# Scan layer: x and B of groups three to seven turned by VectorE blocks and DMAs through DRAM instead of by TensorE

## The chip, the cores and the metric

The kernel runs on one core of one Trainium2 chip. The metric is the device time of one execution in microseconds (us), taken as the median of several runs. TensorE (PE) multiplies matrices, VectorE (DVE) and ScalarE (ACT) do elementwise work, GpSimd (POOL) and SyncE (SP) issue DMAs here. Each engine works through its own instruction list in order; an instruction that waits for another engine or for a DMA holds up everything behind it on its engine.

## What is computed

Two residual layers and a final norm on a 512 x 1024 activation in f32. The first layer is a scan layer (SSD), the second an attention layer (MLA). The change touches the first one alone, cut here to what matters:

```python
proj = u @ in_w                                   # 1024 -> z (2048), x (2048), B (1024), C (1024), dt (32)
xbc  = silu(causal_depthwise_conv(proj[x, B, C]))
xdt  = x * dt                                     # heads of 64, 4 heads to a group, 8 groups, state 128
# in chunks of 128 positions, group by group:
cb     = C @ B^T                                  # per chunk
y_diag = (cb * decay) @ xdt
states = B^T @ (decay_to_end * xdt)               # one 128 x 64 state per head and chunk
y_off  = C @ (state entering the chunk) * exp(a_cum)
out    = gated_group_rms_norm(y_diag + y_off + d_skip * x, z) @ out_w
```

## The kernel before

**Layout.** Activations are kept turned: channels on the 128 partitions, the 512 positions along the free axis. Every product of the large projections is made in three passes (`whi*ah`, `whi*al`, `wlo*ah`) of 8 matmuls of 128x512, 24 matmuls for one 128-column slice of a weight. ACT casts a weight slice to its high part (`whi`, L272) and DVE subtracts to get the low part (`wlo`, L273). There are two `raw` buffers for loaded slices, three for `whi` and three for `wlo`; so the cast of a slice waits until the product two slices before the one now starting has ended, and it stands at the start of a product.

**Groups.** The scan runs over 8 groups, `g` = 0 to 7 (the first to the eighth). While the scan work of group g is done, TensorE's main feed is the projection of group g+1 (`ssm_in`): six products of 24 matmuls in the order B, C, x0, x1, z0, z1. When a product has ended, ACT reads its result (L608) and DVE adds three shifted multiples (the convolution, L610, three dependent steps).

**Order of the work.** TensorE's order is the order of the program. `sched` (L237) walks through the feed, counts 0.216 us for a matmul, and puts in the scan's pieces where the count passes the piece's number: `P1 = (1.0, 2.4, 3.8, 12.0, 18.2)` for `cb`, `x(0)`, `x(1)`, `states` and `y`; the group's norm (`gnorm`, the matmuls `pssq`) of the group before stands at 16.84. The count goes up in steps of 1.296 (six matmuls); 12.0 is passed after 60 matmuls. On the other engines, the DMA queues among them, a scheduler decides the order when the kernel is built.

**The scan's pieces for a group** (class `SSD`): `cb` (L64) turns three 128x128 blocks of B on TensorE (L71) into PSUM, ACT copies them out as `BT` (L73), then C·B (L77), the mask, and the product with the four decay tiles `L` (L81). `x(j)` (L83) turns four blocks of x on TensorE (L89); DVE multiplies by dt straight out of PSUM (`xdt`, L92) and by the decay to the end (`xw`, L94). `states` (L98) is three matmuls `aux<-xw,BT` (L105), followed by five short DVE operations for the running state `S` (L109 to L113). `y` (L116) is the products with `S` (L130) and with `xdt` (L138), and DVE's sums.

**DMAs.** SP issues all loads: weight slices (512 KB, L263), the broadcast rows `L<-ac_d` (L627) and `E<-ea_d` (L123, L124). In the second layer the program already turns a 512 x 1024 tensor in the way that the change uses: eight 128x512 operations that turn 32x32 blocks on DVE (L681), each followed by four DMAs of 64 KB that put the blocks in their places in DRAM (L684, pieces of 32 numbers, 128 bytes).

Of the kernel before, what the change touches and what calls it, by code (L numbers as in the profile page):

```python
# [10 lines left out]
F32 = mybir.dt.float32  # L11
# [4 lines left out]
P = 128  # L16
T = 512
D = 1024
KD = D // P
NCH = T // P  # L20
# [17 lines left out]
SU = (0.64, 1.42)  # L38
P0 = (6.0, 6.8, 11.91, 15.25, 17.25, 24.88, 34.5)
P1 = (1.0, 2.4, 3.8, 12.0, 18.2)  # L40
GN = 16.84
G7 = 33.0
SF = (0.02, 0.1, 2.1, 3.1)
# [11 lines left out]
class SSD:  # L55
# [8 lines left out]
    def cb(self):  # L64
        nc, net, wk, v = self.nc, self.net, self.wk, self.nc.vector
        B, C = self.st["B"], self.st["C"]
        ch = lambda ap: ap.rearrange("p (c s) -> p c s", c=NCH)
        pb = net.ssd_aux()
        for c in range(3):
            s = slice(c * P, (c + 1) * P)  # L70
            nc.tensor.transpose(pb[:, s], B[:, s], net.ident)  # L71
        self.BT = wk.tile([P, 3 * P], F32, tag="BT", name=net.nm("BT"), bufs=1)
        nc.scalar.copy(self.BT[:], pb[:, :3 * P])  # L73
        pc = net.ssd_aux()
        for c in range(NCH):
            s = slice(c * P, (c + 1) * P)
            nc.tensor.matmul(pc[:, s], B[:, s], C[:, s], start=True, stop=True)  # L77
        cb = wk.tile([P, T], F32, tag="cb", name=net.nm("cb"), bufs=2)
        v.tensor_tensor(ch(cb[:]), ch(pc[:]), net.triu[:, None, :].to_broadcast([P, NCH, P]), op=ALU.mult)
        for L in self.L:  # L80
            v.tensor_tensor(L[:], L[:], cb[:], op=ALU.mult)  # L81

    def x(self, j):  # L83
        nc, net, wk, v = self.nc, self.net, self.wk, self.nc.vector
        x = self.st[f"x{j}"]
        px = net.ssd_aux()
        for c in range(NCH):
            s = slice(c * P, (c + 1) * P)
            nc.tensor.transpose(px[:, s], x[:, s], net.ident)  # L89
        h0 = 4 * self.g + 2 * j  # L90
        xp = wk.tile([P, NCH, 2, 64], F32, tag="xdt", name=net.nm("xdt"), bufs=2)
        v.tensor_tensor(xp[:], px[:].rearrange("p (c h d) -> p c h d", c=NCH, h=2),  # L92
                        self.dt[:, :, h0:h0 + 2].unsqueeze(3).to_broadcast([P, NCH, 2, 64]), op=ALU.mult)
        v.tensor_tensor(self.xw[:, :, 2 * j:2 * j + 2, :], xp[:, :3],  # L94
                        self.dend[:, :3, h0:h0 + 2].unsqueeze(3).to_broadcast([P, 3, 2, 64]), op=ALU.mult)
        self.xdt.append(xp)
# [55 lines left out]
class Net:  # L152
# [8 lines left out]
    def build(self):  # L161
        tc, nc, ctx = self.tc, self.nc, self.ctx
        pool = lambda name, bufs, **k: ctx.enter_context(tc.tile_pool(name=name, bufs=bufs, **k))
        self.const = pool("const", 1)
        self.wraw = pool("wraw", 2)
        self.whi = pool("whi", 3)
        self.wlo = pool("wlo", 3)
        self.act = pool("act", 8)
        self.o16 = pool("o16", 16)
        self.nrm = pool("nrm", 1)  # L170
        self.res = pool("res", 8)
        self.dram = pool("dram", 1, space=bass.MemoryType.DRAM)

        const = self.const
        self.xs = []
        self.cols = const.tile([P, C_N], F32, name="cols")
        self.ident = const.tile([P, P], F32, name="ident")[:]
        self.rows = const.tile([P, 2 * NH], F32, name="rows")

        self.phase, self.group, self.before, self.head = "", [], [], None  # L180
        self.wq = []
        self.wpos = self.wload = 0
        self.wraws = []
        self.wready = {}
        for g in range(NG):
            for i in range(6):
                self.wq.append(("w", U_IN + 6 * g + i))
        for i in range(16):
            self.wq.append(("w", U_OUT0 + i))
        for i in range(6):  # L190
            self.wq.append(("w", U_M1 + i))
        self.wq += [("w", U_MZ + i) for i in range(3)] + [("ua", 0), ("w", U_MZ + 3), ("ub", 0), ("uc", 0), ("w", U_MZ + 4)]
        out = [("w", U_OUT1 + i) for i in range(16)]
# [12 lines left out]
        with tc.tile_pool(name="ps_m", bufs=1, space=bass.MemoryType.PSUM, reuse_waits="tile") as ps, \  # L206
                tc.tile_pool(name="mla", bufs=2, reuse_waits="tile") as wk:
            self.ps, self.wk = ps, wk
            self.mla()
# [50 lines left out]
    def load_weight(self, kind, idx):  # L260
        n = {"w": 1024, "ua": 1024, "ub": 640, "uc": 512}[kind]
        raw = self.wraw.tile([P, n], F32, tag="raw", name=self.nm("raw"))
        self.nc.sync.dma_start(raw[:], self.t[kind][idx])  # L263
        return raw

    def split_weight(self, raw, cuts=()):
# [70 lines left out]
    def sumsq(self, tiles, n, pstag, pool=None, tags=("r0", "rt", "rr"), after=None):  # L337
        nc = self.nc
        acc = None
        for x in tiles:  # L340
            sq = self.nrm.tile([P, T], F32, tag="sq", name=self.nm("sq"), bufs=SQ)
            i = nc.scalar.activation(sq[:], x, AF.Square)
            if after is not None:
                self.link(i, [after])
            if acc is None:
                acc = self.nrm.tile([P, T], F32, tag="sqa", name=self.nm("sqa"))
                nc.vector.tensor_scalar(acc[:], sq[:], self.eps_of(n), None, op0=ALU.add)
            else:
                nc.vector.tensor_tensor(acc[:], acc[:], sq[:], op=ALU.add)
        pool = pool or self.nrm  # L350
        hi = pool.tile([P, T], F32R, tag=tags[0], name=self.nm("sqh"))
        lo = pool.tile([P, T], F32R, tag=tags[1], name=self.nm("sql"))
        nc.scalar.copy(hi[:], acc[:])
        nc.vector.tensor_tensor(lo[:], acc[:], hi[:].bitcast(F32), op=ALU.subtract)
        ps = self.ps.tile([P, T], F32, tag=pstag, name=self.nm("pssq"), bufs=self.bufs[pstag])
        nc.tensor.matmul(ps[:], self.onesr[:], hi[:], start=True, stop=False)
        nc.tensor.matmul(ps[:], self.onesr[:], lo[:], start=False, stop=True)
        return ps[:]

    def ssm(self):  # L360
        tc, nc, t, wk = self.tc, self.nc, self.t, self.wk
# [33 lines left out]
        for k in range(KD):  # L395
            a = self.o16.tile([P, T], F32R, tag="o", name=self.nm("vh"))
# [32 lines left out]
            ul.append(b)  # L429

        gn = []
        self.silus(0)
        for g in range(NG):
            ys, q = [], []
            pieces = [] if g == 0 else [(GN, late)]
            if g == 0:
                begin = lambda: q.append(SSD(self, 0, self.lexp(0), ys))
                pieces += [(SU[0] + SU[1] * k, scaled) for k in range(KD)]
                pieces += [(P0[0], step), (P0[1], step), (P0[1] + 0.1, begin)]
                at = P0[2:]  # L440
            else:
                q.append(SSD(self, g, self.lexp(g), ys))
                at = P1
            pieces += [(at[0], lambda: q[0].cb()), (at[1], lambda: q[0].x(0)), (at[2], lambda: q[0].x(1)),
                       (at[3], lambda: q[0].states()), (at[4], lambda: q[0].y())]
            if g + 1 < NG:
                mid = (vh, vl, lambda: r, MID) if g == 0 else (uh, ul, None, 0)
                self.sched(self.ssm_in(g + 1, uh, ul, mid), pieces)
                self.silus(g + 1)
                late = functools.partial(lambda g, ys: gn.extend(self.gnorm(g, ys)), g, ys)  # L450
            else:
                self.part = []
                pieces.append((G7, lambda: gn.extend(self.gnorm(g, ys))))
                self.sched(self.out_half(gn, 0, U_OUT0, [t["x"][k] for k in range(KD)]), pieces)
# [616 lines left out]
```

## Time and profile before

| | |
|---|---|
| time, median of 3 runs | 836.59 us (835.94 to 836.82) |
| the profiled execution | 836.13 us; its span, first to last instruction, 834.0 us |
| busy: PE | 819.3 us, 98% of the span |
| busy: DVE | 644.9 us, 77% |
| busy: ACT | 450.4 us, 54% |
| busy: POOL | 0.2 us |
| granted TensorE clock, mean | 0.999 |

How to read the views in what follows. A row of the timeline has the start in us, the duration, the engine, the line of the kernel, the operation, output<-inputs, and `xN` where N equal operations follow each other (then the duration runs from the first start to the last end). What stands in brackets is the idle time of the engine before the row and what ended it. Durations overlap a little on DVE and ACT: a next operation that does not depend on the last starts about 0.08 us before its end. In the chain of waits a row has start, duration and work. Lines are those of the kernel before.

### The profile page before, as it was taken

To read this page: it belongs to the slowest core of one execution; us is meant where nothing else is said; L and a number is where in the kernel's file an instruction comes from. 1 tells how busy PE (TensorE), PEld (TensorE's weight loads), DVE (VectorE), ACT (ScalarE), POOL (GpSimd) and SP (SyncE) were. 2 spreads that over 40 slices of the span, in tenths; PEclk is the share of its full clock that TensorE was granted. 3 is DMA by queue.
4 is the path that set the end of the run, shared out by engine and by line. 5 is a ranking of instruction groups with operands and counts; after the bars stand their busy time and mean duration, and the time that the engine had idled before them with its cause. 6 is when DMAs were issued, how large, how long until landed. Compare 5 with 4: busy or idle time off the path is not lost.

```text
span 834.0 us, 11549 instructions
## 1 busy us (share of the span) xinstructions
PE 819.3 (98%) x4228; PEld 691.8 (83%) x4228; DVE 644.9 (77%) x1234; ACT 450.4 (54%) x794; POOL 0.2 (0%) x4
## 2 busy tenths in 40 slices
PE   7999999999999999999999999999999999999996
PEld 5887888888888888888888888888888888888885
DVE  7999898979787989778566787786767869675544
ACT  7567755545465657434353654556547557554233
POOL 0000000000000000000000000000000000000000
PEclk9999999999999999999999999999999999999999
DMA  6364543423242423333555142222222224331212
GB/s 227 103 191 141 155 147 106 152 99 129 101 139 90 152 76 127 115 121 94 130 130 132 54 130 64 79 72 76 63 64 58 90 78 152 101 97 56 86 66 101
DMA packets 50856, 90.55 MB, mean 109 GB/s; under 512 B 21552, under 2 KB 23088, under 8 KB 50800
## 3 DMA queue, kind: packets, MB, share of 16 engines
q1 hardware_dynamic: 50080, 88.77, 34.0%
q10 hardware_dynamic: 720, 1.05, 0.3%
q8 instruction: 33, 0.54, 0.3%
q14 instruction: 23, 0.19, 0.1%
HBM read 83.12 MB, written 4.33 MB: 105 GB/s over the span
## 4 chain that ended last, share of the span: by engine, by line
PE 92%; DVE 3%; DMA 2%; ACT 1%; SPq 1%; issue 0%; DVEq 0%; ACTq 0%
PE mm L291 55%; PE ot L941 11%; PE s L793 5%; PE mm L300 4%; PE po L835 4%; PE mm L773 3%; PE pt L817 2%; PE yd L138 2%; PE yd L291 1%; PE aux L130 1%; PE aux L105 1%; DMA x<-in_x_dram 1%; PE aux L77 1%; PE aux L89 1%; DMA L<-ac_d 1%; DVE wlo L273 1%
## 5 line engine op out<-in xcount | busy, mean ns | idle before, releaser
L272 ACT CAST whi<-raw 128x1024 fp32r<-128x1024 f32 (+3 forms) x132 | 127.0, 965 | 210.3 <-PE mm L291 172.8
L273 DVE TENSOR_TENSOR wlo<-raw,whi 128x1024 fp32r<-128x1024 f32 (+3 forms) x132 | 146.8, 1115 | 54.6 <-ACT whi L272 54.3
L291 PE MATMUL mm<-ah,whi 128*128 128x512 f32 x384 | 154.0, 401 | 0.0
L291 PE MATMUL mm<-ah,wlo 128*128 128x512 f32 x384 | 150.3, 391 | 0.4 <-DVE wlo L273 0.4
L291 PE MATMUL mm<-al,whi 128*128 128x512 f32 x384 | 149.9, 390 | 0.0
L291 PE MATMUL mm<-vh,whi 128*128 128x512 f32 x224 | 89.4, 399 | 0.8 <-ACT whi L272 0.8
L291 PE MATMUL mm<-vh,wlo 128*128 128x512 f32 x224 | 87.9, 392 | 0.7 <-DVE wlo L273 0.7
L291 PE MATMUL mm<-vl,whi 128*128 128x512 f32 x224 | 87.6, 391 | 0.0
L291 PEld LDWEIGHTS mm<-ah,wlo 128*128 128x128 f32 x384 | 72.1, 188 | 16.1 <-DVE wlo L273 0.8
L291 PEld LDWEIGHTS mm<-ah,whi 128*128 128x128 f32 x384 | 72.2, 188 | 15.3 <-issue 1.4
L291 PEld LDWEIGHTS mm<-al,whi 128*128 128x128 f32 x384 | 72.2, 188 | 14.4 <-DVE al L312 0.3
L941 PE MATMUL ot<-whi,ah 128*128 128x512 f32 (+1 forms) x136 | 52.4, 385 | 0.0
L941 PE MATMUL ot<-whi,al 128*128 128x512 f32 (+1 forms) x136 | 51.5, 379 | 0.0
L941 PE MATMUL ot<-wlo,ah 128*128 128x512 f32 (+1 forms) x136 | 51.4, 378 | 0.0
L291 PEld LDWEIGHTS mm<-vh,wlo 128*128 128x128 f32 x224 | 42.1, 188 | 10.7 <-DVE wlo L273 1.5
L291 PEld LDWEIGHTS mm<-vh,whi 128*128 128x128 f32 x224 | 42.2, 188 | 9.4 <-ACT whi L272 1.1
L223 ACT ACTIVATE p<-p,st 128x128 f32<-128x128 f32 (+1 forms) x64 | 36.1, 564 | 25.3 <-DVE st L805 25.2
L291 PEld LDWEIGHTS mm<-vl,whi 128*128 128x128 f32 x224 | 42.2, 188 | 7.3
L821 ACT CAST ph<-pt 128x512 fp32r<-128x512 f32 (+1 forms) x64 | 26.4, 421 | 33.3 <-PE pt L817 32.8
L291 PE MATMUL mm<-ch,whi 128*128 128x512 f32 x104 | 42.6, 410 | 0.0
L291 PE MATMUL mm<-ch,wlo 128*128 128x512 f32 x104 | 40.9, 393 | 0.0
L291 PE MATMUL mm<-cl,whi 128*128 128x512 f32 x104 | 40.8, 392 | 0.0
(223 smaller groups left out, 1637.7 us busy)
## 6 DMA issues: line engine op xcount, KB each, us to landing
raw<-in_w_dram SPq DMA_DIRECT2D x100, 512.0 KB, 3.3
L<-ac_d SPq DMA_DIRECT2D x32, 256.0 KB, 3.9
E<-ea_d SPq DMA_DIRECT2D x32, 128.0 KB, 3.5
raw<-in_ua_dram SPq DMA_DIRECT2D x8, 512.0 KB, 3.3
raw<-in_ub_dram SPq DMA_DIRECT2D x8, 320.0 KB, 2.8
x<-in_x_dram SPq DMA_DIRECT2D x8, 256.0 KB, 4.4
res<-in_x_dram SPq DMA_DIRECT2D x8, 256.0 KB, 3.1
hd<-ht SPq DMA_DIRECT2D x32, 64.0 KB, 3.5
```

The lines of the kernel that those rows point to most:

```text
L138: nc.tensor.matmul(yd[64 * h:64 * h + 64, s], self.xdt[j][:, c, h, :], self.L[2 * j + h][:, s], start=True, stop=True)
L223: i = self.nc.scalar.activation(out, in_, func, **k)
L272: nc.scalar.copy(hi[:, a:b], raw[:, a:b])
L273: nc.vector.tensor_tensor(lo[:, a:b], raw[:, a:b], hi[:, a:b].bitcast(F32), op=ALU.subtract)
L291: self.nc.tensor.matmul(ps, a, b, start=i == 0, stop=i == len(seq) - 1)
L300: self.nc.tensor.matmul(p, seq[i][0], seq[i][1], start=i == 0, stop=i == 3 * ks - 1)
L773: nc.tensor.matmul(ps[:, c2 * 256:(c2 + 1) * 256], a, b, start=i == 0, stop=i == 5)
L793: nc.tensor.matmul(ps[:, :n], x[:, s], y[:, :n], start=k == 0, stop=k == 4)
L817: nc.tensor.transpose(pt[:, (b - kb) * P:(b - kb + 1) * P], probs[h][b][:, kb * P:(kb + 1) * P], self.ident)
L821: nc.scalar.copy(ph[:, :n], pt[:, :n])
L835: nc.tensor.matmul(po[:, kb * P:], x, y, start=kb == 0 and k == 0, stop=kb == NCH - 1 and k == 2)
L941: nc.tensor.matmul(ps[:, a:b], x, y, start=start and i == 0, stop=stop and i == 5)
```

## The change

In groups g = 2 to 6 (the third to the seventh) TensorE no longer turns B and x. Instead:

- `flip` turns 32x32 blocks of x0, x1 and B on DVE (three operations of 128x512) and sends each with four DMAs of SP to a scratch tensor in DRAM, so that the blocks land in turned order: 12 DMAs, in pieces of 128 bytes;
- `back` reads the scratch with three DMAs of SP into `xdt` (two) and `BT`; ACT's copy of `BT` goes;
- `x(j)` multiplies `xdt` in place, from SBUF and not from PSUM;
- the pieces have other numbers: `P2` for groups four to seven, `P3` for the third, in which `states` is put at 15.5 and 19.0 (12.0 before), `y` at 21.0 and 25.0 (18.2 before). 15.5 is passed after 72 matmuls, which is the end of the product x0; 19.0 after 90;
- from the feed of group 1 on, all weight slices to the end of the program are issued by GpSimd (`wqueue`) and not by SP.

```diff
+P2 = (0.2, 1.0, 8.0, 11.5, 11.6, 15.5, 21.0)
+P3 = (0.2, 1.0, 8.0, 13.0, 13.1, 19.0, 25.0)
+FLIP = range(2, 7)
...
     def cb(self):
...
+        if self.g not in FLIP:
...
+    def flip(self):
+        nc, net, wk = self.nc, self.net, self.wk
+        d = net.flip_d[self.g % 2]
+        turned = d[:].rearrange("(j a) n -> a j n", a=32)
+        for m, name in enumerate(("x0", "x1", "B")):
+            t = wk.tile([P, T], F32, tag="u", name=net.nm("tp"), bufs=3)
+            nc.vector.transpose(t[:], self.st[name][:])
+            for i in range(4):
+                n = m * P + 32 * i
+                nc.sync.dma_start(turned[:, :, n:n + 32], t[32 * i:32 * i + 32, :].rearrange("a (j n) -> a j n", n=32))
+
+    def back(self):
+        nc, net, wk = self.nc, self.net, self.wk
+        rows = net.flip_d[self.g % 2][:].rearrange("(c p) n -> p c n", p=P)
+        self.px = []
+        for j in range(2):
+            xp = wk.tile([P, NCH, 2, 64], F32, tag="xdt", name=net.nm("xdt"), bufs=2)
+            nc.sync.dma_start(xp[:].rearrange("p c h d -> p c (h d)"), rows[:, :, j * P:(j + 1) * P])
+            self.px.append(xp)
+        self.BT = wk.tile([P, 3 * P], F32, tag="BT", name=net.nm("BT"), bufs=1)
+        nc.sync.dma_start(self.BT[:].rearrange("p (c n) -> p c n", c=3), rows[:, :3, 2 * P:])
...
     def x(self, j):
...
+        else:
+            xp = self.px[j]
+            px = xp[:]
+        v.tensor_tensor(xp[:], px,
...
-        self.nc.sync.dma_start(raw[:], self.t[kind][idx])
+        self.wqueue.dma_start(raw[:], self.t[kind][idx])
...
+        self.flip_d = [self.dram.tile([T, 3 * P], F32, name=f"flip{i}") for i in range(2)]
...
+                if g in FLIP:
+                    turn, cb, back, *rest = P3 if g == FLIP[0] else P2
+                    at = (cb, *rest)
+                    pieces += [(turn, lambda: q[0].flip()), (back, lambda: q[0].back())]
...
+            if g >= FLIP[0] - 1:
+                self.wqueue = nc.gpsimd
```

The order of the built programs at three places follows. A row has the line, the operation, output<-inputs with buffer numbers, and the shape. Lines are those of the program that the row is from: in the changed kernel `xdt` is L123, `xw` L125, `states` L136, the convolution L649, `wlo` L305, `pssq` L388 and the first step of the norm after it L354.

**TensorE, fifth group, around `states`.** Before: the product x0 of the next group is `mm_2136`, and the states stand within it, after 12 of its 24 matmuls.

```order
L291 MATMUL mm_2136<-al_563,whi_2096 128x512
L291 MATMUL mm_2136<-ah_562,wlo_2097 128x512
L105 MATMUL aux_2149<-xw_2024,BT_2042 128x256 x2
L105 MATMUL aux_2150<-xw_2024,BT_2042 128x256
L291 MATMUL mm_2136<-ah_595,whi_2096 128x512
```

Now: the product x0 is `mm_2152`, the product x1 `mm_2205`.

```order
L323 MATMUL mm_2152<-al_695,whi_2106 128x512
L323 MATMUL mm_2152<-ah_694,wlo_2107 128x512
L136 MATMUL aux_2186<-xw_2038,BT_2133 128x256 x2
L136 MATMUL aux_2187<-xw_2038,BT_2133 128x256
L323 MATMUL mm_2205<-ah_521,whi_2148 128x512
```

The states moved from the middle of the product x0 to the point between x0's last matmul and x1's first.

**VectorE, fifth group, around `xdt` and `xw`.** Before: the decay tiles, the four operations, then the low part of a weight and the convolution of the product B.

```order
L81 TENSOR_TENSOR L_2017<-L_2017,cb_2049 128x512
L92 TENSOR_TENSOR xdt_2066<-aux_2061,dt 128x512
L92 TENSOR_TENSOR xdt_2080<-aux_2075,dt 128x512
L94 TENSOR_TENSOR xw_2024<-xdt_2066,dec 128x3x128
L94 TENSOR_TENSOR xw_2024<-xdt_2080,dec 128x3x128
L273 TENSOR_TENSOR wlo_2133<-raw_2094,whi_2132 128x1024
L610 SCALAR_TENSOR_TENSOR B_2089<-mm_2031,cols,B_2089 128x511
```

Now: `whi_2261` is the cast that waits for the end of the product x0, and `x_389` is what the convolution makes of that product.

```order
L649 SCALAR_TENSOR_TENSOR C_2141<-mm_2110,cols,C_2141 128x509
L305 TENSOR_TENSOR wlo_2262<-raw_2199,whi_2261 128x1024
L649 SCALAR_TENSOR_TENSOR x_389_2181<-mm_2152,cols,x_389_2181 128x511
L649 SCALAR_TENSOR_TENSOR x_389_2181<-mm_2152,cols,x_389_2181 128x510
L123 TENSOR_TENSOR xdt_2129<-xdt_2129,dt 128x512
L649 SCALAR_TENSOR_TENSOR x_389_2181<-mm_2152,cols,x_389_2181 128x509
L125 TENSOR_TENSOR xw_2038<-xdt_2129,dec 128x3x128
L123 TENSOR_TENSOR xdt_2131<-xdt_2131,dt 128x512
L125 TENSOR_TENSOR xw_2038<-xdt_2131,dec 128x3x128
L140 COPY S_2191<-aux_2186 128x256
```

The four operations moved from ahead of the convolution of B to behind the low part and two steps of the convolution that belong to the end of the product x0.

**VectorE, third group, the same four operations.** Before they stand as in the fifth group.

```order
L92 TENSOR_TENSOR xdt_1350<-aux_1345,dt 128x512
L92 TENSOR_TENSOR xdt_1364<-aux_1359,dt 128x512
L94 TENSOR_TENSOR xw_1308<-xdt_1350,dec 128x3x128
L94 TENSOR_TENSOR xw_1308<-xdt_1364,dec 128x3x128
L273 TENSOR_TENSOR wlo_1417<-raw_1378,whi_1416 128x1024
```

Now: `x_259` comes from the product x0 of the next group; `rt_1486` waits for the norm's matmuls `pssq`, which TensorE has after the first six matmuls of the product x1, and for two operations of ACT on them.

```order
L305 TENSOR_TENSOR wlo_1534<-raw_1458,whi_1533 128x1024
L649 SCALAR_TENSOR_TENSOR x_259_1453<-mm_1424,cols,x_259_1453 128x511
L649 SCALAR_TENSOR_TENSOR x_259_1453<-mm_1424,cols,x_259_1453 128x510
L354 SCALAR_TENSOR_TENSOR rt_1486<-pssq_1482,r_270_1485 128x512
L123 TENSOR_TENSOR xdt_1401<-xdt_1401,dt 128x512
L123 TENSOR_TENSOR xdt_1403<-xdt_1403,dt 128x512
L125 TENSOR_TENSOR xw_1310<-xdt_1401,dec 128x3x128
L125 TENSOR_TENSOR xw_1310<-xdt_1403,dec 128x3x128
```

They moved behind the first step of the norm. In the fourth group all four stand between the third step of C's convolution and the `wlo` that waits for the end of x0; in the sixth and seventh the `xdt` and `xw` of x0 stand early, about the `L` products, and only those of x1 stand at C's convolution: on either side of its third step (sixth), or right behind it (seventh). The states of these three groups stand on TensorE as in the fifth, those of the third group after 18 matmuls of the product x1.

More of the change, by code (lines that the diff above doesn't have):

```diff
@@ L67, in cb @@
         ch = lambda ap: ap.rearrange("p (c s) -> p c s", c=NCH)
[L68 to L73, printed above, removed]
+        if self.g not in FLIP:
+            pb = net.ssd_aux()
+            for c in range(3):
+                s = slice(c * P, (c + 1) * P)
+                nc.tensor.transpose(pb[:, s], B[:, s], net.ident)
+            self.BT = wk.tile([P, 3 * P], F32, tag="BT", name=net.nm("BT"), bufs=1)
+            nc.scalar.copy(self.BT[:], pb[:, :3 * P])
         pc = net.ssd_aux()
@@ L81, in cb @@
             v.tensor_tensor(L[:], L[:], cb[:], op=ALU.mult)
+    def flip(self):
[16 more added lines that the diff above has]
+            self.px.append(xp)
+        self.BT = wk.tile([P, 3 * P], F32, tag="BT", name=net.nm("BT"), bufs=1)
+        nc.sync.dma_start(self.BT[:].rearrange("p (c n) -> p c n", c=3), rows[:, :3, 2 * P:])
     def x(self, j):
@@ L85, in x @@
         x = self.st[f"x{j}"]
[L86 to L89, printed above, removed]
         h0 = 4 * self.g + 2 * j
-        xp = wk.tile([P, NCH, 2, 64], F32, tag="xdt", name=net.nm("xdt"), bufs=2)
-        v.tensor_tensor(xp[:], px[:].rearrange("p (c h d) -> p c h d", c=NCH, h=2),
+        if self.g not in FLIP:
+            px = net.ssd_aux()
+            for c in range(NCH):
+                s = slice(c * P, (c + 1) * P)
+                nc.tensor.transpose(px[:, s], x[:, s], net.ident)
+            px = px[:].rearrange("p (c h d) -> p c h d", c=NCH, h=2)
+            xp = wk.tile([P, NCH, 2, 64], F32, tag="xdt", name=net.nm("xdt"), bufs=2)
+        else:
+            xp = self.px[j]
+            px = xp[:]
+        v.tensor_tensor(xp[:], px,
                         self.dt[:, :, h0:h0 + 2].unsqueeze(3).to_broadcast([P, NCH, 2, 64]), op=ALU.mult)
@@ L180, in build @@
         self.phase, self.group, self.before, self.head = "", [], [], None
+        self.wqueue = nc.sync
         self.wq = []
```

## Prediction

> **What bounds the kernel now.** I read first the page's span, busy times and chain, then who made TensorE (PE) wait, then the chain of waits through the fifth group.
>
> ```profile
> span 834.0 us, 11549 instructions
> PE 819.3 (98%) x4228; PEld 691.8 (83%) x4228; DVE 644.9 (77%) x1234; ACT 450.4 (54%) x794; POOL 0.2 (0%) x4
> ```
>
> ```profile
> PE mm L300 <- ACT whi L272: 4.8, 1, 4.8
> ...
> PE aux L105 <- DVE xw L94: 0.6, 1, 0.6
> ```
>
> TensorE is busy for 98% of the span, and the largest wait is the start-up (4.8 us, once). The states (L105) waited for DVE's `xw` once, for 0.6 us. So TensorE's list of work is the time, and two things count: matmul time taken off it is won in full, and a wait put into it is paid in full. The chain through the fifth group, start and duration:
>
> ```profile
> 211.38 0.33 PE aux L71 x3
> ...
> 214.00 0.43 PE aux L89 x4
> ...
> 215.82 0.44 PE aux L89 x4
> ...
> 225.82 1.30 PE aux L105 x6
> 227.12 4.10 PE mm L291 x18
> 231.22 0.23 PE pssq L356
> 231.45 0.23 PE pssq L357
> ...
> 251.50 0.33 PE aux L71 x3
> ```
>
> The turning of B (L71) and of x0 and x1 (L89) lies on the chain. One 128x512 matmul takes 4.10/18 = 0.228 us, a product of 24 takes 5.47. A group lasts 251.50 - 211.38 = 40.1 us; the turning of B stands six matmuls behind its start, which is 210.0. DVE's side of the same group is read from the timeline, ACT's casts beside it:
>
> ```profile
> 216.79 1.28 DVE L92 TENSOR_TENSOR xdt<-aux,dt 128x512 f32<-128x512 f32 x2
> 217.99 1.02 DVE L94 TENSOR_TENSOR xw<-xdt,dec 128x384 f32<-128x384 f32 x2
> ...
> 220.06 2.31 DVE L610 SCALAR_TENSOR_TENSOR B<-mm,cols,B 128x511 f32<-128x511 f32 x3
> 223.99 1.23 DVE L273 TENSOR_TENSOR wlo<-raw,whi 128x1024 fp32r<-128x1024 f32 x1 [1.62 <-ACT whi L272]
> 225.13 1.53 DVE L610 SCALAR_TENSOR_TENSOR C<-mm,cols,C 128x511 f32<-128x511 f32 x2
> 226.72 0.42 DVE L109 COPY S<-aux 128x256 f32<-128x256 f32 x1
> ...
> 230.75 1.23 DVE L273 TENSOR_TENSOR wlo<-raw,whi 128x1024 fp32r<-128x1024 f32 x1 [1.16 <-ACT whi L272]
> 231.89 1.53 DVE L610 SCALAR_TENSOR_TENSOR x<-mm,cols,x 128x511 f32<-128x511 f32 x2
> 233.34 0.68 DVE L322 SCALAR_TENSOR_TENSOR rt<-pssq,r 128x512 f32<-128x512 f32 x1
> 233.93 0.74 DVE L610 SCALAR_TENSOR_TENSOR x<-mm,cols,x 128x509 f32<-128x509 f32 x1
> 234.59 0.68 DVE L323 TENSOR_TENSOR rt<-rt,r 128x512 f32<-128x512 f32 x1
> ```
>
> ```profile
> 222.90 1.05 ACT L272 CAST whi<-raw 128x1024 fp32r<-128x1024 f32 x1 [3.71 <-PE mm L291]
> ...
> 229.66 1.05 ACT L272 CAST whi<-raw 128x1024 fp32r<-128x1024 f32 x1 [5.03 <-PE mm L291]
> ```
>
> The reader is to see three things. `xw` was ready at 219.0, about 7 us ahead of the states. A `wlo` is not free to run early: DVE stood idle for 1.62 and 1.16 us ahead of two of them, since the cast waits for the end of a product (222.90 is the end of C, 229.66 the end of x0). And the copy L109 sits between the second and third step of C's convolution, which is its place in the built program's list too: DVE keeps its list, whatever is ready behind.
>
> **What is removed.** Per group 0.33 + 0.43 + 0.44 = 1.20 us of TensorE, in five groups 6.0 us. ACT's copy of `BT` is off the chain and is worth nothing.
>
> **What is added on DVE and the queues.** The second layer has both new operations:
>
> ```profile
> L681 DVE STREAM_TRANSPOSE ht<-res x8: 699/711/712, 388.2 to 431.6; 128x512 f32<-128x512 f32 x8
> ```
>
> ```profile
> L684 SPq DMA_DIRECT2D hd<-ht x32: 341/487/856, 389.0 to 448.9; - x32
> ...
> DMA to landing us min/median/max: 2.3/3.5/3.7
> ```
>
> ```profile
> 213.00:253.00 40.00, 40.00 (x216) 33.58 (x215) 34.04 (x61) 22.20 (x35) 0.00 (x0) 1.00 0.35 119
> ```
>
> ```profile
> L<-ac_d SPq DMA_DIRECT2D x32, 256.0 KB, 3.9
> ```
>
> Three turns of 0.71 us are 2.1 us a group on a DVE that is busy for 34.04 of 40.00 us: there is room. A round trip is 3 x 0.71 on DVE, 12 issues of 0.49 = 5.9 us on SP, 3.5 to land, and 3.9 for the read (256 KB, as `L`): 15.4 us one after the other, and it starts about at the group's start (the operands are ready by then; in the fifth group the turns stand on DVE ahead of `cb`). The first `xdt` is read on DVE 16.2 us after the group's start at the earliest (C's end 222.90 - 210.0, less the 1.2 removed, and 4.46, below), and `BT`, the last to land, is needed later still; the issues also overlap the turns and each other's landing. I take 0, with a cover of a few us. Queued behind it on SP are only `L` and `E`, which need the group before to have finished, and weight slices no longer stand there. The multiplication by dt from SBUF instead of PSUM I take at the same 0.68 us.
>
> **What is added on TensorE: waits for `xw`.** The states need all of `xw`. I follow DVE's new list with the rows above.
>
> *Fifth group.* The states stand right behind the product x0, and DVE has the `wlo` of x0's end and two convolution steps of x0 ahead of `xdt`. From that end (229.66 in the rows): `wlo` starts at +1.09; the convolution at +2.23; where `rt` stood, at +3.68, now comes the first `xdt`; the third step at +4.27; the first `xw` at +4.93 (0.66 on); the second `xdt` 0.47 later (1.02 for two), at +5.40; it takes 0.68, the second `xw` 0.55 more: +6.63, with signals **6.7 us**. TensorE has nothing else in its list: it stands for all of that.
>
> *Fourth group.* The states stand at the same place, but DVE has only C's work ahead. From C's end (222.90): `wlo` +1.09, convolution from +2.23, three steps 2.31, to +4.54; `xdt` and `xw` of x0 from +4.46, `xw` at +5.14, `xdt` of x1 at +5.61, `xw` from +6.29 to +6.84. TensorE arrives one product after C's end, at +5.47: a wait of **1.4**.
>
> *Third group.* The states stand 18 matmuls and `pssq` behind x0's end: 18 x 0.228 + 0.46 = +4.56. DVE has `rt` at +3.68 as before, then two `xdt` from +4.27, two `xw` from +5.47, done at +6.49: **1.9**.
>
> *Sixth and seventh.* One `xdt` and one `xw` at the end of C's steps: `xw` done at about +5.5 and +5.74 against +5.47: 0 and **0.3**.
>
> Together 6.7 + 1.4 + 1.9 + 0.3 = 10.3 us. `y` follows the states' start by 1.30 + 30 x 0.228 + 0.46 = 8.6 us; where DVE has all of this between, it needs 1.1 + 1.2 (`wlo`), three convolution steps and two norm steps at 0.7, and five `S` operations at 0.42: 7.9. I take no second wait, and up to 0.5 a group at the high end.
>
> **TensorE's clock after the long wait.** The trace shows the clock falling and rising:
>
> ```profile
> 4.79 0.80 PE L300 MATMUL mm<-vh,whi 128*128 128x512 f32 x1 [4.79 <-ACT whi L272]
> ...
> 8.87 0.58 PE L300 MATMUL mm<-vh,whi 128*128 128x512 f32 x1
> 9.29 0.39 PE L300 MATMUL mm<-vl,whi 128*128 128x512 f32 x1
> ```
>
> ```profile
> 826.45 0.28 PE L941 MATMUL ot<-wlo,ah 128*128 128x256 f32 x1
> ```
>
> ```profile
> 830.00:832.00 2.00, 0.00 (x0) 0.00 (x0) 0.00 (x0) 0.00 (x0) 0.00 (x0) 0.97 1.04 384
> 832.00:834.00 2.00, 0.00 (x0) 0.00 (x0) 0.00 (x0) 0.00 (x0) 0.00 (x0) 0.50 0.22 80
> ```
>
> The last matmul ends at 826.73; a mean clock of 0.97 up to 832 puts the fall to half at 831.9, after 5.2 us without work. After a start the first ten matmuls took 9.29 - 4.79 = 4.50 us instead of 2.28: 2.2 us lost. A wait of 6.7 us is longer than 5.2, so I add **2.2 us** once (0 if it does not fall, up to twice that if it rises late). The Trainium skill, "TensorE: Matmul & The Clock Gate", section "Part 1: The HAM clock gate", says that the clock is halved after an idle window of about 3.4 us and restored after a busy one, the windows running freely; the rows agree with 5.2 and 4.4 us. By that rule alone a wait of 6.7 us holds a whole window nearly always, and at least 3.4 us at half speed would cost about 1.6, an estimate.
>
> **The weight slices on GpSimd's queue.** No DMA of that queue is in the trace. SP's own loads land after
>
> ```profile
> DMA to landing us min/median/max: 2.5/3.3/7.0
> ```
>
> and the tightest of a group has 6.5 us, from its issue to the end-of-group cast:
>
> ```profile
> 243.44 0.34 SPq L263 DMA_DIRECT2D raw<-in_w_dram  x1
> ```
>
> ```profile
> 249.95 1.05 ACT L272 CAST whi<-raw 128x1024 fp32r<-128x1024 f32 x1 [2.85 <-PE mm L291]
> ```
>
> That leaves 3.2 us, and a late cast still has two products (10.9 us) less 1.05 and 1.23 before TensorE needs it. Nearest row 3.3, far end 7.0: I take 0, and up to 1.5 us for single late loads; a gain is excluded where TensorE does not wait for loads. If a load had to stand while DVE runs scalar operations within SBUF, the longest run of those in a group is this:
>
> ```profile
> 244.80 2.24 DVE L634 TENSOR_SCALAR L<-L,ac 128x128 f32<-128x128 f32 x11
> ```
>
> 2.24 us is inside the 3.2. The Trainium skill, "SBUF — State Buffer", section "SBUF: two separate sides", warns of this: a DMA issued by GpSimd cannot get its descriptors written while DVE runs an operation that takes both ports. No run so far shows it; by that rule the last rival has its chance.
>
> **The sum.** 836.13 (profiled: 834.0 of span and 2.1 around it) - 6.0 + 10.3 + 2.2 = 842.6. The median of the runs before lies 0.46 above that execution, so the forecast for the median is 836.59 + 6.5 = **843.1 us**.
>
> **The rivals.**
> - *The clock stays up* (slower, smaller): 836.6 - 6.0 + 10.3 = 840.9. For it: the fall was seen once, and the margin over 5.2 us is 1.5. Chance 0.20; with the fall, the forecast, 0.62.
> - *The other side, faster:* `xw` is there when TensorE comes, and only the 6.0 us are left: 830.6. The place is DVE's list ahead of the fifth group's states; it decides when `xdt` runs 6.7 us earlier there, ahead of the `wlo`. For it: the turned data are in SBUF by then, and the states were moved 2.7 us later (12 matmuls). Against it: the L109 row, DVE keeps its list. Chance 0.08, and 0.03 that waits and gains cancel (within 0.2%, 1.7 us, about what a measurement of this kernel can tell).
> - *The round trip is late:* if pieces of 128 bytes take twice 15.4 us beside the weights, `xdt` waits in all five groups, some 12 us each in place of the waits above: 836.6 - 6.0 + 60 = about 890. Against it: the same DMAs land after at most 3.7. Chance 0.02.
> - *GpSimd's loads are slow:* two `raw` buffers serve two slices in 13.4 us (40.1 us a group, six slices), less cast and low part 2.3: beyond about 11 us a load, TensorE runs at the loads' pace, and single waits start beyond 7. At 8 us I put it at 847, at 12 us far higher. Chance 0.05.
>
> **The numbers.** Slower 0.62 + 0.20 + 0.02 + 0.05 = 0.89, the same 0.03, faster 0.08. The low end is the rival without the fall less 1 us for DVE steps that overlap better: 839.9. The high end is the sum with a clock that stays low twice as long (2.2) and 1.5 for late loads: 846.8. Left out are 0.08 + 0.03 below and 0.07 above, and little of the rest.
>
> **What would show it.** Right: TensorE waits at the states for DVE's `xw`, four times, 6.7, 1.4, 1.9 and 0.3 us, the long one in the fifth group; matmuls of 0.43 us spacing behind it; no L71 and L89 in five groups. Wrong: no such wait, or one that ended on a DMA; a cast of a weight that waited for a load; DVE rows in another order than the list.

## The result, and the profile after

The changed kernel takes 846.02 us (median of 4 runs, 845.71 to 847.69), the kernel before beside it on the same chip 836.71 us (835.94 to 838.93): a ratio of 1.0111, 95% interval 1.0088 to 1.0134. It is slower by 9.3 us; the forecast was slower by 6.5 us. Ratios here and below are of executions at nearly full clock: one execution each of experiments 9 and 10 ran at a granted clock of 0.66, took 1166 us and is not in them.

The page's first lines and TensorE's waits in the changed kernel (what waited, for what: us in total, times, longest):

```profile
span 843.9 us, 11617 instructions
...
PE 815.8 (97%) x4173; PEld 687.1 (81%) x4173; DVE 653.2 (77%) x1249; ACT 448.6 (53%) x789; POOL 60.1 (7%) x116
```

```profile
PE aux L136 <- issue: 9.9, 3, 6.6
PE mm L332 <- ACT whi L304: 4.7, 1, 4.7
...
PE mm L323 <- DVE al L344: 1.5, 1, 1.5
```

TensorE has 55 instructions fewer (4173 against 4228, the turning of five groups), yet the span grew by 9.9 us. The states (L136) now wait 9.9 us in three places, and a wait of 1.5 us for `al` (L344), the low part of a scan output, is new. "issue" means that this view found nothing that ended the wait; VectorE's (DVE's) timeline shows what did. First the chain of waits, around the states of the third, fourth, fifth and seventh group:

```profile
152.46 1.83 issue
154.29 1.53 PE aux L136 x6
...
188.82 1.50 issue
...
229.39 6.56 issue
235.95 2.90 PE aux L136 x6
238.84 2.10 PE mm L323 x6
...
246.90 1.34 PE aux L161 x12
...
316.12 0.19 issue
316.31 1.53 PE aux L136 x6
```

and DVE's timeline in the fifth group:

```profile
230.26 1.22 DVE L305 TENSOR_TENSOR wlo<-raw,whi 128x1024 fp32r<-128x1024 f32 x1 [1.98 <-ACT whi L304]
231.41 1.53 DVE L649 SCALAR_TENSOR_TENSOR x<-mm,cols,x 128x511 f32<-128x511 f32 x2
232.85 0.68 DVE L123 TENSOR_TENSOR xdt<-xdt,dt 128x512 f32<-128x512 f32 x1
233.45 0.74 DVE L649 SCALAR_TENSOR_TENSOR x<-mm,cols,x 128x509 f32<-128x509 f32 x1
234.11 0.55 DVE L125 TENSOR_TENSOR xw<-xdt,dec 128x384 f32<-128x384 f32 x1
234.57 0.68 DVE L123 TENSOR_TENSOR xdt<-xdt,dt 128x512 f32<-128x512 f32 x1
235.29 0.56 DVE L125 TENSOR_TENSOR xw<-xdt,dec 128x384 f32<-128x384 f32 x1
```

The second `xw` ends at 235.85, TensorE goes on at 235.95. DVE stood idle for 1.98 us ahead of a `wlo` while the two reads of `xdt`, issued from 220.78 on and 3.5 and 5.1 us on the way, were there by 226.5, over 6 us ahead of the first `xdt`: the list, not the data, made this wait. The waits are 1.83, 1.50, 6.56, 0 and 0.19 us.

TensorE's clock in the same place (stretch, busy time, granted clock, DMA share, GB/s):

```profile
233.00:234.00 1.00, 0.00 (x0) 0.71 0.91 221
...
239.00:240.00 1.00, 1.00 (x4) 0.50 0.00 0
240.00:241.00 1.00, 1.00 (x5) 0.87 0.00 0
```

A mean of 0.71 puts the fall at 233.42, 4.0 us into the wait, and 0.87 the rise at 240.26: 6.8 us at half speed. From the states to `y` it took 246.90 - 235.95 = 10.95 us; at full clock the same rows last 1.53 + 1.38 + 0.46 + 5.47 = 8.84. The fall cost 2.1 us: of the 6.8, 2.5 lay within the wait, and the 4.3 behind it did half their work.

The place that the prediction has no term for is the start of the eighth group, where the feed changes to the output product. The chain there, changed kernel:

```profile
326.51 1.90 PE yd L169 x32
...
343.94 2.49 DVE L L85 x4
346.43 0.61 DVE al L344
...
347.09 8.92 PE mm L323 x38
```

TensorE needs the last `al`, and DVE's list has the four products `L * cb` (L85) ahead of it, which need the eighth group's `L`. Its loads go out when `y` has read the old `L`. Timeline, SP and DVE (L673 works on `L` ahead of its exponential):

```profile
327.56 1.76 SPq L666 DMA_DIRECT2D L<-ac_d  x4
...
336.81 0.88 DVE L673 TENSOR_SCALAR L<-L,ac 128x128 f32<-128x128 f32 x4 [1.10 <-DMA L<-ac_d]
337.60 4.30 DVE L344 TENSOR_TENSOR al<-y,ah 128x512 fp32r<-128x512 f32 x7
```

The four loads took 3.5 to 7.8 us to land. DVE waited for the last of them, and from 336.81 to the end of the last `al` its timeline shows no gap. (The chain itself reaches `L * cb` over ACT, whose exponentials of `L` ended at 343.92, at the same time as DVE got there.)

The seventh group's product of C and B stood at 291.95 us in the kernel before and stands at 300.24 now, 8.3 later; the loads of `L` went out at 317.06 and go out at 327.56, 10.5 later. Relative to TensorE's work they lost 2.2 us, and before there was no wait behind them.

### The profile page after: what moved, and what is told of

It reads as the page before. It is cut to its first block, busy times and chain, and to the rows that moved or that the text cites. A ratio compares the mean times of both kernels' runs of the same rounds, so it can differ in the third digit from the quotient of the medians.

```text
span 843.9 us, 11617 instructions
## 1 busy us (share of the span) xinstructions
PE 815.8 (97%) x4173; PEld 687.1 (81%) x4173; DVE 653.2 (77%) x1249; ACT 448.6 (53%) x789; POOL 60.1 (7%) x116
## 3 DMA queue, kind: packets, MB, share of 16 engines
q1 hardware_dynamic: 72912, 41.25, 18.2%
## 4 chain that ended last, share of the span: by engine, by line
PE 88%; DVE 5%; DMA 3%; issue 2%; ACT 2%; SPq 1%; DVEq 0%; ACTq 0%
PE mm L323 52%; PE ot L980 10%; PE s L832 5%; PE mm L332 4%; PE po L874 4%; PE mm L812 3%; PE pt L856 2%; PE yd L169 2%; PE aux L136 1%; PE yd L323 1%; PE aux L161 1%; DMA x<-in_x_dram 1%; DVE wlo L305 1%; DMA L<-ac_d 1%; PE aux L81 1%
## 5 line engine op out<-in xcount | busy, mean ns | idle before, releaser
L305 DVE TENSOR_TENSOR wlo<-raw,whi 128x1024 fp32r<-128x1024 f32 (+3 forms) x132 | 146.5, 1113 | 46.8 <-ACT whi L304 46.3
L295 POOL DMA_DIRECT2D raw<-in_w_dram x88 | 47.0, 534 | 623.1 <-DVE wlo L305 377.8
L323 PEld LDWEIGHTS mm<-vh,whi 128*128 128x128 f32 x224 | 42.1, 188 | 10.1 <-ACT whi L304 1.8
```

Of the source, the lines that this page charges most:

```text
L295: self.wqueue.dma_start(raw[:], self.t[kind][idx])
L305: nc.vector.tensor_tensor(lo[:, a:b], raw[:, a:b], hi[:, a:b].bitcast(F32), op=ALU.subtract)
L323: self.nc.tensor.matmul(ps, a, b, start=i == 0, stop=i == len(seq) - 1)
```

## The experiments

Each kernel was timed beside the kernel before (medians 836.5 to 836.9 us in these comparisons); ratios carry their 95% intervals. The main theory: the time is TensorE waiting for DVE's list, plus the clock once, plus the eighth group's start. The rivals are named in each expectation. They were written from a reading in which 1.4 us of waiting for `whi` were put to the eighth group's start; that wait stands in the first 60 us, and only the 1.5 us for `al` belong there.

### 1. The queue alone

```diff
-        self.nc.sync.dma_start(raw[:], self.t[kind][idx])
+        self.wqueue.dma_start(raw[:], self.t[kind][idx])
...
+            if g >= 1:
+                self.wqueue = nc.gpsimd
```

> The kernel before, with all weight slices from the feed of group 1 on issued by GpSimd. Theory (the change's time is TensorE's waits for DVE's xw in the fifth, fourth and third group, the clock at half once, and a wait of 2.9 us at the eighth group's start that comes from the later y): the queue costs nothing, 836.7 us, within 0.7. Rival, the queue: the loads of GpSimd come late and make the 2.9 us at the eighth group's start, 839.6.

Measured: 836.94 us, ratio 1.0001 (0.9992 to 1.0010). In itself GpSimd's queue costs nothing that shows; the interval leaves room for 0.7 us less to 0.8 us more. Its loads land 0.2 us later than SP's 3.3:

```profile
raw<-in_w_dram POOLq DMA_DIRECT2D x88, 512.0 KB, 3.5
```

### 2. The seventh group's y alone, later

```diff
-                at = P1
+                at = (*P1[:4], 21.0) if g == NG - 2 else P1
```

> The kernel before, with y of the seventh group alone at 21.0 instead of 18.2; nothing is flipped, all loads stay on SP. Theory: the loads of L for the eighth group can start only when y has read the old L, they come 2.7 us later, and TensorE waits at the eighth group's start for whi and al: between 1.3 and 2.9 us, so 838.0 to 839.6. Rival (the wait comes from the queue of GpSimd, or from the many small packets): 836.7 as before.

Measured: 837.94 us, ratio 1.0010 (1.0002 to 1.0019), so 1.0 us more. The wait for `al` appears without any flip, and the chain now runs from `y` through the loads of `L`:

```profile
PE mm L291 <- DVE al L312: 0.8, 1, 0.8
```

```profile
321.36 5.12 DMA L<-ac_d
```

The mechanism is the expected one; the size (1.3 to 2.9 us) was put too high, for the reason named above.

### 3. The turning left out

```diff
+        if self.g in range(2, 7):
+            self.BT = B
...
+        px = x
+        if self.g not in range(2, 7):
```

> The kernel before, with the turning of B and x left out in groups three to seven and nothing in its place: states and y use B and x unturned, so the scan's products there are not the reference's. Theory: every matmul taken off TensorE is won in full, 5 x 1.20 = 6.0 us, 830.7. Rival (the turning filled time in which TensorE would wait for something else): 832.5 or more, with new waits at the states, at y or at the eighth group's start.

Measured: 830.72 us, ratio 0.9924 (0.9911 to 0.9938): 6.2 us. From `y` to `y` a group lasts 309.78 - 270.94 = 38.84 us (rows below), against 314.67 - 274.55 = 40.12 before: 1.28 each, 6.4 us for five.

```profile
270.94 1.34 PE aux L135 x12
...
309.78 1.34 PE aux L135 x12
```

This kernel is also a check on noise. Up to the third group its engines' lists are those of before, and yet the second group's `y` began at 114.07 us in the profile of before and at 115.61 here (114.95 in the changed kernel); the first 60 us hold a wait of 1.3 us for a `whi` here, of 1.4 in the changed kernel and of 0.6 in before. In the thirteen profiles of this case it began between 114.07 and 115.61, earliest in that of before. So I put the 0.9 us by which the changed kernel was behind there, of the 9.9 between the two spans, down to chance at the start; that is argued, not shown.

### 4. DVE's list in the fifth group alone

```diff
+            s = nc.vector.tensor_tensor(lo[:, a:b], raw[:, a:b], hi[:, a:b].bitcast(F32), op=ALU.subtract)
+            if self.wpos in WHOLD:
+                self.link(s, [self.xw_ops[self.wpos // 6 - 1, j] for j in range(2)])
...
+                if name in HOLD and g - 1 in AHEAD:
+                    self.link(s, [self.xw_ops[g - 1, j] for j in range(2)])
```

with `AHEAD = (4,)`, `HOLD = ("x0",)`; `WHOLD` names the slice whose cast waits for x0's end, and `link` only orders two instructions of one engine.

> The changed kernel; in the fifth group alone DVE's list is forced to have xdt and xw ahead of the convolution of x0 and of the low part that belongs to x0's end. Theory: the wait at the states of the fifth group falls from 6.56 to about 1.4 us, as in the fourth, and the clock no longer falls there (2.1 us): 846.0 - 5.2 - 2.1 = 838.7. Rival, late data: xdt is not there earlier, the wait and the time stay, 846.0. Rival, no clock term: the 2.1 us stay in another form, 840.8.

Measured: 838.31 us, ratio 1.0017 (1.0009 to 1.0026), 7.7 us less than the changed kernel. Chain, fifth group:

```profile
231.10 1.38 issue
232.49 1.53 PE aux L141 x6
234.02 1.40 PE mm L331 x6
```

The wait is 1.38 and the clock stays up. The two traces have the same order of work on every engine but DVE, so no transfer was changed: late data is ruled out for this wait. But the same profile has a surprise in the third group, behind a wait of 1.84 us (152.44 to 154.27) like the one in the changed kernel:

```profile
154.00:155.00 1.00, 0.73 (x3) 0.79 0.00 0
155.00:156.00 1.00, 1.00 (x4) 0.50 0.06 16
...
158.00:159.00 1.00, 1.00 (x6) 1.00 0.00 0
```

The clock fell at 154.58 and rose at 158.0, after a wait of less than 2 us. The edit can't have made this, since up to there the two kernels' lists are the same. From the states to `y` it took 10.04 us (154.27 to 164.31), against 8.39 in the changed kernel (154.29 to 162.68).

### 5. The weight slices back on SP

```diff
-                self.wqueue = nc.gpsimd
+                self.wqueue = nc.sync
```

> The changed kernel with the weight slices left on SP's queue, as before. The scheduler then lists DVE's work otherwise: in the fifth group xdt and xw stand ahead of the low part and the convolution of x0, in the third and fourth a little later than in the changed kernel. Theory (DVE's list sets the waits): the fifth group's wait of 6.56 and the clock's 2.1 go, the third and fourth wait 3.1 and 2.3 instead of 1.83 and 1.50: 846.0 - 6.6 - 2.1 + 2.1 = 839.4. Rival, the queue: weight slices stand behind twelve flips on SP, casts come late, TensorE waits for them: 846 or more.

Measured: 837.55 us, ratio 1.0013 (1.0000 to 1.0025), 8.5 us less than the changed kernel. The states waited 2.98 us (third group) and 2.15 (fourth), with the clock at half for 3.4 us behind each, and not at all in the fifth:

```profile
219.40 14.98 PE mm L323 x66
234.38 1.30 PE aux L136 x6
```

DVE's timeline shows why: the first `xdt` stands ahead of the `L * cb` now, and the second `xw` is done at 233.3:

```profile
220.04 0.68 DVE L123 TENSOR_TENSOR xdt<-xdt,dt 128x512 f32<-128x512 f32 x1
...
232.02 0.68 DVE L123 TENSOR_TENSOR xdt<-xdt,dt 128x512 f32<-128x512 f32 x1
232.73 0.56 DVE L125 TENSOR_TENSOR xw<-xdt,dec 128x384 f32<-128x384 f32 x1
```

So the queue, worth nothing that shows by itself, decided 8.5 us here, most of it because the scheduler laid out another list for DVE. SP's other transfers also land sooner in this run (`L` after 4.0 us against 4.8, flips after 2.8 against 4.0), and the wait for `al` is 0.2 us; what share of that last gain is the list and what the landing was not separated.

### 6. The seventh group's states and y early

`AHEAD = (6,)`, with `HOLD = ("C", "x0")` and the numbers

```diff
+PA = (0.2, 1.0, 7.5, 7.6, 7.7, 13.0, 18.2)
```

> The changed kernel; in the seventh group alone states and y go back to 13.0 and 18.2, and DVE's list is forced to have xdt and xw ahead of the convolution of C there. It is flipped as the others are. Theory (the later y holds up the loads of L): the wait for al at the eighth group's start, 1.5 us, falls to 0.3 or less; a wait of about 0.6 us at the seventh states in place of 0.19: 846.0 - 1.2 + 0.4 = 845.2. Rival (packets and queues of the flips make it): the 1.5 us stay, 846.4.

Measured: 844.48 us, ratio 1.0094 (1.0081 to 1.0107), 1.5 us less than the changed kernel. All sixty flips are still there, and the wait for `al` is gone:

```profile
PE mm L331 <- DVE al L352: 0.2, 1, 0.2
```

The fall behind a short wait came again: the states of the third group waited 1.83 us, and the clock was at half for 3.4 us behind it.

Together with experiment 2, this shows that the wait for `al` needs the late `y` (experiment 7, where `y` stands at 18.2 too, has 0.2 as well). Flips don't make it: none is under way there. But the place of `y` alone doesn't set the length. The four loads of `L` took 3.5 to 7.8 us to land in the changed kernel (wait 1.5), 4.7 to 6.4 in experiment 2 (wait 0.8), 3.3 to 4.7 here, and 3.5 to 4.8 in experiment 5, where `y` stands late and the wait is 0.2. In the changed kernel GpSimd issued a weight slice of 512 KB at 328.04, among these loads; whether that is what slowed them was not tested.

### 7. Longer waits: y early, DVE's list late

```diff
-P2 = (0.2, 1.0, 8.0, 11.5, 11.6, 15.5, 21.0)
+P2 = (0.2, 1.0, 8.0, 11.5, 11.6, 15.5, 18.2)
```

> The changed kernel with y at 18.2 instead of 21.0 in groups four to seven; DVE's list then has xdt and xw behind the low part and the convolution of x0 in the sixth and seventh group too, with waits at the states of about 5.9 us each beside the 6.56 of the fifth. Theory: two more long waits, 11.6 us, the clock falls in each of them, 4.2 us, and the wait for al goes, 1.5: 860.3. Rival, the clock fell in the fifth group by chance of phase: 856 to 858. Rival, al waits for something else than the later y: 1.5 more.

Measured: 860.43 us, ratio 1.0288 (1.0273 to 1.0302). The waits at the states of the fifth, sixth and seventh group are 6.56, 5.79 and 5.78 us; the sixth in the chain:

```profile
276.47 5.79 issue
282.25 2.90 PE aux L136 x6
...
290.62 1.34 PE aux L161 x12
```

The states last 2.90 us behind each of the three, as behind the long wait of the changed kernel: the clock fell in all of them. From the states to `y` it took 7.83, 8.37 and 8.66 us; at full clock 1.53 + 1.38 + 0.46 + 2.75 = 6.12, so 1.7, 2.3 and 2.5 us were lost. The long wait of the changed kernel did not lose its 2.1 us by an accident of phase.

### 8. Waits of 2 us

All five groups with `AHEAD`, states and `y` at the old numbers:

```diff
+PA = (0.2, 1.0, 7.5, 7.6, 7.7, 12.0, 18.2)
```

> All five groups flipped, DVE's list forced as in best_a, but states at 12.0 (in the middle of the product x0) and y at 18.2 in every group, so that TensorE comes about 2 us too early for xw or BT five times. Question: the clock. In earlier runs it fell for 3.4 us after a wait of 1.84, of 2.15 and of 2.98 us, costing 1.6 us each, and did not fall after others of 1.5 to 1.9. Theory, that a wait of about 2 us costs the clock in some executions and not in others: 836.9 - 6.4 + 10 = 840.5 without a fall, up to 848.5 with five, and the single runs differ by more than 2 us. Rival, a fixed threshold above 3 us, the earlier falls having another cause: 840.5, and a clock that is up throughout.

Measured: 841.98 us, ratio 1.0078 (1.0062 to 1.0094). Four runs lie at 841.3 to 842.1, two at 845.0 and 845.3. The profiled run, one of the four, has five waits of 1.9 us and no fall. The 3.3 us between the two sets of runs fit two falls of 1.65. No profile shows them as rows, but the mean granted clock of each execution does: 0.998 in the four, 0.994 in the two. A stretch of 3.4 us at half speed takes 1.7 of some 840 us, 0.002, off that mean, so the two executions had two falls more. This is the expected theory, not the rival of a fixed threshold above 3 us: the same program loses the clock in some executions and not in others. The third group's wait says the same: it is 1.83 or 1.84 us in the profiles of the changed kernel and of experiments 4, 6 and 7, whose lists are alike up to there, and the clock fell in 4 and 6 alone. What decides it is open.

### 9 to 11. Keeping the gain

Experiment 9 has `AHEAD` in all five groups, so that the convolutions of C and x0 and the low part of x0's end no longer stand ahead of `xw`:

```diff
+PA = (0.2, 1.0, 7.5, 7.6, 7.7, 15.5, 22.1)
+PZ = (0.2, 1.0, 7.5, 7.6, 7.7, 13.0, 18.2)
```

(`PZ` for the seventh group.)

> All five groups flipped; DVE's list is forced to have xdt and xw ahead of C's and x0's convolution in each; states at 15.5 and y at 22.1 in groups three to six, 13.0 and 18.2 in the seventh. Theory: no wait at the states but 0.6 us in the seventh group, no fall of the clock, the turning is won: 836.9 - 6.4 + 0.6, plus 0.2 for each of four groups whose states stand at a product's end, plus 0.3 at the eighth group's start: 832.2. Rival, late data: the round trip through DRAM with its small packets is what xdt waits for as soon as DVE's list no longer hides it, several us in each group: 842 or more.

Measured: 835.35 us, ratio 0.9981 (0.9973 to 0.9990). Now the data are late:

```profile
PE aux L142 <- DVE xw L130: 2.7, 2, 1.5
PE aux L142 <- DMA BT<-flip: 2.6, 2, 1.4
```

TensorE waited for `BT` on its way back from DRAM in two groups. Its read is the last of fifteen DMAs that SP issues for a group; the twelve flips alone took 9.1 us in the fifth. Experiment 10 puts the flips of x1, and the read of x1, on GpSimd:

```diff
+                (nc.gpsimd if name in ("x1",) else nc.sync).dma_start(turned[:, :, n:n + 32], ...)
...
+            (nc.gpsimd if j else nc.sync).dma_start(xp[:].rearrange("p c h d -> p c (h d)"), ...)
```

> As best_a, with one more edit: the four flips of x1 and the read that brings x1 back are issued by GpSimd, the others by SP. Theory: in best_a the twelve issues on SP, 6 to 9 us, made BT land after TensorE had come to the states, 1.2 and 1.4 us in two groups, and xdt in the seventh, 1.3; with eight issues on SP and four on GpSimd all of it lands about 2 us earlier, and the three waits go or shrink to 0.4: 835.4 - 3.5 = 831.9. Rival, the transfers themselves are slow and not the issues: the waits stay, 835.4.

Measured: 835.66 us, ratio 0.9985 (0.9975 to 0.9995), no better. `BT` no longer keeps TensorE waiting, but in the sixth group `xw` was 2.1 us late, 1.2 of it a wait of DVE for the second `xdt`, and the clock fell for 3.4 us behind it. GpSimd's list says why (in brackets the idle time before):

```profile
259.07 0.55 POOL L302 DMA_DIRECT2D raw<-in_w_dram  x1 [5.53 <-DVE wlo L312]
259.69 0.76 POOL L109 DMA_DIRECT2D xdt<-flip  x1
```

The read of `xdt` stood behind a weight slice that had to wait for its buffer. Experiment 11 keeps the flips of x1 on GpSimd and takes that read back to SP:

> As best_a, with the four flips of x1 issued by GpSimd, but all reads back on SP. In the run before, the read of the second xdt stood on GpSimd behind a weight slice that waited 5.5 us for a wlo, which made xw late by 2.1 us in the sixth group and 1.3 in the seventh; on SP it stands behind the first xdt's read and eight flips. Theory (the round trip lands in time once neither queue holds it): no wait at the states in groups three to six, 0.6 us in the seventh: 836.6 - 6.4 + 0.6 + 0.8 (the states at a product's end) + 0.3 = 831.9. Rival (the four flips on GpSimd themselves come too late, behind its weight slices): waits of 1 to 2 us stay in two groups, 835.

Measured: 832.41 us (832.11 to 834.91), ratio 0.9956 (0.9944 to 0.9968): 4.1 us faster than the kernel before and 13.6 faster than the change. Its profile shows three waits of 0.8 to 1.1 us left, in the fifth, sixth and seventh group (the fourth of the row, 1.4, is the second group's and not flipped):

```profile
PE aux L142 <- DVE xw L130: 4.3, 4, 1.4
```

## Why the prediction was right, and where it was not

**The turning removed.** Put at 6.0 us, it is 6.4 (experiment 3). Each stretch of three or four turnings also cost about 0.03 us around it that the three rows didn't hold.

**Waits for xw.** Put at 1.9, 1.4, 6.7, 0 and 0.3 us, together 10.3; measured 1.83, 1.50, 6.56, 0 and 0.19, together 10.08. The walk through the new list with the durations of before was good to 0.15 us a group, and experiment 4 shows that the list was the cause of the largest. What the prediction didn't ask is which edit made the list: experiment 5 shows that the fifth group's goes away when nothing but the queue of the weight slices is put back.

**The clock.** Put at 2.2, measured 2.1. That they are so close is partly luck, since experiment 7 has 1.7 to 2.5 us for the same; and the step behind it was only half right. "A wait of 6.7 us is longer than 5.2" took the one fall in the trace of before as a threshold; the fall came 4.0 us into the wait, and experiments 4, 5, 6 and 10 show falls behind waits of 1.84, 2.15 and 2.98, 1.83 and 2.07 us. The rival in which the clock stays up was wrong for this wait, and experiment 7 shows it for two more. The Trainium skill, "TensorE: Matmul & The Clock Gate", section "Part 1: The HAM clock gate", has freely running windows of about 3.4 us: the low stretches of 6.8 and 3.4 us here are two of them and one. That an idle window is needed for the fall, as it says, these runs don't bear out: in a window of 3.4 us a wait of 1.84 leaves 1.6 us of work.

**The round trip, taken at 0.** Right for the changed kernel, where DVE's list is later than the data everywhere. The 16.2 us to the first `xdt` hold for the fifth group, not for all: in the sixth and seventh, x0's `xdt` stands about the `L` products (at 263.39 in the sixth, 2.2 us after the product of C and B). The data were there because x0's flips go out before the group starts (from 246.98, read back from 257.38, at most 4.4 us to land). Its cover was thinner than "a few us": with the list out of the way, `BT` came 1.2 and 1.4 us late (experiment 9).

**GpSimd's queue, taken at 0.** Right by itself (experiment 1, ratio 1.0001); loads landed after 3.5 us, so of the warning in the Trainium skill, "SBUF — State Buffer", section "SBUF: two separate sides", about DMAs issued by GpSimd these runs show at most 0.2 us. Wrong in company, through the list (experiment 5).

**The step that failed** is "I take no second wait". It looked at `y` in its own group and found 7.9 of 8.6 us used, which held. It did not follow `y` to the next group: `y` frees the `L` buffers, the loads of `L` wait for that, `L * cb` waits for the loads, and in the eighth group alone `al` stands behind `L * cb` in DVE's list with TensorE waiting for it. The prediction even named `L` as what is queued behind on SP, and stopped there. It cost 1.5 us at the `al` row, part of it because these loads landed late, and the stretch from the seventh group's `y` to the eighth's states grew by 0.4 more that is not placed.

**A small term** was left out though the trace of before had it. In the chain the states count 1.53 us behind a wait, not 1.30. The trace fits a first weight load that is then not hidden: it starts 0.03 us ahead of the row in the seventh group (316.28, 316.31), and 0.23 ahead where the states did not wait (225.42, 225.65 in the kernel before). In the timeline, where the states that did not wait last 1.46 us, the row of those that waited 0.63 us in the kernel before reads

```profile
78.47 1.56 PE L105 MATMUL aux<-xw,BT 128*128 128x256 f32 x6 [0.63 <-DVE xw L94]
```

Some 0.2 us in each of five groups are 1.1 (the sixth, whose `xw` came just in time, had 1.48). It is not the place at a product's end, as the expectation of experiment 9 had it: in experiment 11 the third group's states stand there without a wait and last 1.30. The sum with measured terms: -6.4 + 10.1 + 2.1 + 1.9 + 1.1 = 8.8, which is what the two profiles differ by between the second group's `y` and the eighth's states ((356.01 - 114.95) - (346.34 - 114.07) = 8.8). Most of these terms were read from the same two profiles, so the sum says that no other large term is missing, not that each is proved. The medians differ by 9.3; the last half microsecond is not placed.

**Where the number landed.** The forecast was 843.1 us; the time is 846.02, near the high end of the range, 846.8. That it lies inside is luck: the range was stretched upwards for a clock that stays low twice as long (2.2 us) and for late loads of weights (1.5), and neither came. The two terms that were missing, 1.9 and 1.1 us, used that room.

## What to carry to other kernels

Where a scheduler lays out the lists, walk through the built list of the engine that others wait for, after every edit: an edit that is free by itself, like a queue, can reorder another engine. Follow a moved step to the next user of each buffer that it frees, past the end of its own group. Work taken off the bounding engine is won in full only if the replacement's whole path, issues in their queue included, ends before that engine comes.

## What the runs showed of the hardware

- TensorE's granted clock fell to half behind waits of 1.83, 1.84, 2.07, 2.15 and 2.98 us, for 3.4 us each, at about 1.6 us of lost time; other waits of 1.5 to 1.9 us, the same one of the third group among them, cost nothing but themselves.
- Waits of 5.8 and 6.6 us took the clock down every time seen (five of five: once in the changed kernel, once in experiment 6, three times in experiment 7), for 1.7 to 2.5 us more.
- A weight slice of 512 KB landed after 3.5 us from GpSimd's queue and 3.3 from SP's, and held GpSimd for 0.53 us.
